# Three sums over partitions: one f32 product replaced by two products of rounded parts

## The chip, the core and the metric

The kernel runs on one core of one Trainium2 chip, as one launch. The metric is the device time of that launch in microseconds; three runs of the kernel before gave 1331.88 to 1332.85 us, median 1332.03 us. The core has five engines that work side by side and meet only at semaphores: PE (TensorE, matrix products), ACT (ScalarE), DVE (VectorE), POOL (GpSimd) and SP (SyncE, which here does nothing but issue DMAs). Each engine takes its instructions strictly in the order in which they stand in its list, so an instruction that waits holds up everything behind it on that engine.

## The reference, cut to what matters

Two layers over a residual stream x of 1024 tokens by 1024 channels, in float32:

```python
for i in range(2):
    h = rms_norm(x, norm_g[i])
    x = x + (conv_branch(h) if i == 0 else attention_branch(h))
    gate = sigmoid(rms_norm(x, ple_norm_g[i]) @ ple_w_gate[i])   # embedding gate
    x = x + (p[i] @ ple_w_proj[i]) * gate

def rms_norm(x, g):
    return x * rsqrt(mean(x * x, axis=-1) + 1e-6) * g
```

There are five mean squares over the channels: the input norm of layer 0 and of layer 1, the norm of each of the two embedding gates, and the layer norm inside the convolution branch (with a mean beside it). The change concerns three: the two gates' and layer 1's input norm.

## The kernel before, in words

The kernel keeps x channel-major: 8 tiles of 128 channels (partitions) by 1024 tokens. A mean square over channels is then a sum over tiles (adds of squares into one 128x1024 tile, on POOL and DVE) followed by a sum over the 128 partitions. That last sum is a product on PE with a 128x128 matrix of ones, which also broadcasts the result to all partitions. `ones_sum` (L186) does it in two halves of 512 tokens. The ones are the right half of the constant tile `cst` (128x256 f32, identity and ones side by side); its load is one of five in `consts` (L363).

All large products are done with operands split in two rounded parts: `hi_of` (L165, ACT) rounds a tile to the type fp32r, `lo_of` (L171, or L173 with a scale; DVE or POOL) subtracts that from the original, and `gemm_k` (L175) multiplies hi·hi, hi·lo and lo·hi on PE (L181). The sums over partitions were the exception: they multiply f32 tiles as they are.

The program goes through these stages: the convolution branch's input product (`bacc`, `aacc`; weights `wraw` and `raw`, input tiles `xt`), the depthwise convolution, its output product (`oacc`), the gate of layer 0 (`gacc`, one unit for each of 8 output tiles; sum `ssb2` in `ple_stat`, L694), layer 1's attention (its first tile of work, products `pqk` and `pv` of weights `raww`, runs before the norm `rstd1`, L819, whose sum is `ssb3`), the attention's output product (`oacc3`), and the gate of layer 1 (sum `ssb4`).

What sets the order: the lists of PE, ACT, DVE and POOL are written out by the code. In the convolution stages and at the gates, `Order` (L116) collects small functions with a due time each and runs them sorted by it; within a function the instructions stand as written. The constants come at -8, ahead of the first weight split at T_X - 1. SP's list alone is ordered by a scheduler, which puts each load where it expects its buffer to be free. Buffers come from pools by tag: the tag X has 8 buffers of 128x1024 at layer 0's gate (`pt`, `pj`, `xi`, `rt`, `rb3` and the squares take them in turn) and 7 at layer 1's.

At a gate, `rstd` (L200) turns the sum into a reciprocal root (DVE L205, ACT's logarithm and exponential L206 and L207, DVE L209 to L215), and `ple` (L712) evicts each unit: DVE multiplies the product by it (L715), ACT takes the sigmoid (L716), DVE multiplies by the projected embedding `pj` (L718), POOL adds x (`xi`, L719), ACT and DVE split the result (`h2hi`, `h2lo`). The logarithm and the sigmoid need different tables on ACT, so an ACT_TABLE_LOAD stands ahead of each.

Of the kernel before, what the change touches and what calls it, by code (L numbers as in the profile page):

```python
# [11 lines left out]
F32 = mybir.dt.float32  # L12
F32R = mybir.dt.float32r
# [9 lines left out]
P = 128  # L23
S = 1024
# [15 lines left out]
    pe=[0, 0, 1, 0, 1, 0, 1, 0],  # L40
# [56 lines left out]
TB, PB = 4, 3  # L97
# [14 lines left out]
def f(ap):  # L112
    return ap.bitcast(F32)
# [18 lines left out]
def kernel(ctx: ExitStack, tc: tile.TileContext, a, out):  # L132
    nc = tc.nc
    act, dve, pool, pe = nc.scalar, nc.vector, nc.gpsimd, nc.tensor
    ctx.enter_context(tc.manual_schedule(engines={ENG.PE, ENG.Activation, ENG.DVE, ENG.Pool}))

    cp = ctx.enter_context(tc.tile_pool(name="const", bufs=1))
# [10 lines left out]
    cst = cp.tile([P, 2 * P], F32, name="cst")  # L148
    vec = cp.tile([P, 7, KT], F32, name="vec")
    ident, ones = cst[:, :P], cst[:, P:]  # L150
    r1 = cp.tile([P, 24], F32, name="r1")
    r64 = cp.tile([P, 24], F32, name="r64")
    ct = cp.tile([P, 24, 2, 16], F32, name="ct")
# [3 lines left out]
    def dma(dst, src):  # L157
        nc.sync.dma_start(dst, src)
# [4 lines left out]
    def hi_of(hi, src, scale=None):  # L163
        if scale is None:
            act.activation(hi, src, AF.Copy)  # L165
        else:
            act.activation(hi, src, AF.Copy, scale=scale)

    def lo_of(lo, src, hi, scale=None, eng=None):
        if scale is None:  # L170
            (eng or dve).tensor_sub(lo, src, f(hi))  # L171
        else:
            dve.scalar_tensor_tensor(lo, src, scale, f(hi), op0=ALU.mult, op1=ALU.subtract)  # L173
# [10 lines left out]
    halves = [slice(0, 512), slice(512, S)]  # L184
    whole = [slice(0, S)]

    def ones_sum(mk, *xs):

        accs = []
        for c in halves:  # L190
            acc = mk()
            for i, x in enumerate(xs):
                pe.matmul(acc, ones, x[:, c], start=i == 0, stop=i == len(xs) - 1)
            accs.append(acc)
        return accs

    def hv(x):
        return [x[:, h] for h in halves]

    def rstd(rb, accs, t, xm, out=None):  # L200

        act.preload_act_table_set("natural_log_exp_and_others")
        both = list(zip(rb, accs, t, xm))
        for r, acc, t, x in both:
            dve.tensor_scalar(x, acc, 1.0 / D, EPS, op0=ALU.mult, op1=ALU.add)  # L205
            act.activation(t, x, AF.Ln)  # L206
            act.activation(r, t, AF.Exp, scale=-0.5)  # L207
        for r, acc, t, x in both:
            dve.tensor_mul(t, r, r)  # L209
        for r, acc, t, x in both:  # L210
            dve.tensor_mul(t, t, x)
        for r, acc, t, x in both:
            dve.tensor_scalar(t, t, -0.5, 1.5, op0=ALU.mult, op1=ALU.add)
        for (r, acc, t, x), y in zip(both, out or rb):
            dve.tensor_mul(y, r, t)  # L215
# [21 lines left out]
    def chunk(o, t, mk, w, xh, xl, nk, dt=1.3, ready=None):  # L237

        acc = {}
        for k in range(nk):  # L240
            def step(k=k):
                if k == 0:
                    acc["a"] = mk()
                gemm_k(acc["a"], (w["h"], w["l"]), xh, xl, k, nk)
            if ready:
                t = max(t, ready[k] - k * dt)
            o.at(t + k * dt, step)
        return t + nk * dt, acc
# [21 lines left out]
    def tok(x, g, t):  # L270

        if g == 0:
            b, c = divmod(t, 4)
            return x.rearrange("p (l c a b) -> p l c a b", l=8, c=4, b=2)[:, :, c, :, b]
        if g == 1:
            r, b = divmod(t, 2)
            return x[:, 256 * r + b : 256 * r + 256 : 2]
        return x[:, t * P : t * P + P]
# [5 lines left out]
    def n_half(x, h):  # L284

        return (x[:, 512 * h : 512 * h + 512].rearrange("p (c l a) -> p c l a", c=4, l=8),
                lambda y: y.rearrange("p (l c a b) -> p c l a b", l=8, c=4, b=2)[..., h])
# [5 lines left out]
    xp = l0.enter_context(tc.tile_pool(name="xp", bufs=1))  # L293
    wp = l0.enter_context(tc.tile_pool(name="wp", bufs=1))
# [7 lines left out]
    def G(name, dt=F32):  # L302
        return gp.tile([P, S], dt, name=name, tag="G", bufs=16)

    def X(name, n=S):
        return xp.tile([P, n], F32, name=name, tag="X", bufs=8)

    def mm(name):
        return ps.tile([P, S], F32, name=name, tag="mm", bufs=2)

    def half(name):
        return ps.tile([P, 512], F32, name=name, tag="half", bufs=2)
# [3 lines left out]
    parts = [{}, {}]  # L316
# [33 lines left out]
    def p_out(i, n, acc, eng):  # L350
        r = X("pout") if i else G("pout")
        eng(r, acc)
        dma(proj_d[i][n], r)
# [9 lines left out]
    def consts():  # L363
        rv["all"] = carry.tile([P, S], F32, name="rope", tag="c")
        at_ = 0
        for nm, n in (("pos", 24), ("invf", 8), ("ggk", 2 * HD), ("posf", 24), ("ang", 192), ("n1", 192), ("n2", 192), ("sin", 192)):
            rv[nm] = rv["all"][:, at_ : at_ + n]
            at_ += n
        rv["pos"] = rv["pos"].bitcast(I32)
        rv["ggk"] = rv["ggk"].rearrange("p (a b) -> p a b", a=2)  # L370
        dma(cst, a["cst"])
        dma(dw, a["dw"])
        for nm in ("pos", "invf", "ggk"):
            dma(rv[nm], a[nm])
# [86 lines left out]
    def stat0():  # L461
        rstd(hv(rb0), ones_sum(lambda: half("ssb"), sv["q", 0]), hv(X("rt")), hv(sv["q", 0]))
# [5 lines left out]
    t = T_X + 2.5  # L468
    T_y = []
    for n in range(KT):  # L470
        if n in P_AT:
            i = P_AT.index(n)
# [14 lines left out]
        dt = 1.3 if n else 2.8  # L487
# [106 lines left out]
    def mean():  # L594
        sv["mb"] = ones_sum(lambda: half("mb"), sv["s1"], dch[7])
# [60 lines left out]
    for n in range(KT):  # L656

        tn = T_o
        if n < 2:
            w = weights(o, wp, a["w_cout"][n], KT, T_o + 4 * n, dve)  # L660
            te, acc = chunk(o, tn + 0.1 * n, (lambda: mm("oacc")) if n else (lambda: hv(ps.tile([P, S], F32, name="oacc0", tag="eA", bufs=1))),
                            w, yh, yl, KT, 2.6, ready)
            if n:
                T_o = te
        else:
            w = weights(o, wp, a["w_cout"][n], KT, tn)
            te, acc = chunk(o, tn, lambda: mm("oacc"), w, yh, yl, KT)
# [24 lines left out]


    def ple_stat(mk, X, s):  # L694
        acc = ones_sum(mk, s["q", 0])
        s["rb"] = X("rb3")
        rstd(hv(s["rb"]), acc, hv(X("rt")), hv(s["q", 0]))

# [27 lines left out]
    for n in range(KT):  # L726
        tn = T_e + C * n + (1.8 if n else 0)
        w = weights(o, wp, a["w_pg"][0, n], KT, tn)
        te, acc = chunk(o, tn, lambda: mm("gacc2"), w, gh, gl, KT)
# [31 lines left out]
    wk = tc.alloc_tile_pool(name="wk", bufs=1, side="right", reuse_waits="tile")  # L761
# [7 lines left out]
    def wk_k(w, raw, eng=None):  # L769

        hi, lo = (wk.tile(list(raw.shape), F32R, name=f"wk{p}", tag=f"wk{next(slot) % WKB}", bufs=1) for p in "hl")
        if eng:
            eng.tensor_copy(hi, raw)
        else:
            hi_of(hi, raw)
        w[0].append(hi)
        w[1].append(lo)
        return lambda eng=dve: lo_of(lo, raw, hi, eng=eng)
# [3 lines left out]
    for k in range(KT):  # L782
        if k > 4:
            raws[k] = wk_raw(a["w_ain"][0], 768, k)
        lo = wk_k(w, raws[k])
# [31 lines left out]
    rbg = s3["q", 0]  # L817

    def rstd1():  # L819

        for acc, c in zip(ones_sum(lambda: pt_("ssb3", "t", TB), rbg), halves):
            dve.tensor_scalar(rbg[:, c], acc, 1.0 / D, EPS, op0=ALU.mult, op1=ALU.add)
        m = pt_("ms", "t", TB, (P, 24))
        row = [kp.tile([1, 512], F32, name="row", tag="P", bufs=PB) for _ in range(2)]
        for h in range(2):
            act.copy(row[h].rearrange("p (c l a) -> p c l a", c=4, l=8), n_half(rbg, h)[1](rbg[0:1]))
        for g in (2, 1, 0):
            for t in range(8):
                x = tok(rbg[0:1], g, t) if g else row[t // 4][:, t % 4 * P : t % 4 * P + P]
                pe.transpose(m[:, 8 * g + t : 8 * g + t + 1], x, ident[0:1, 0:1])  # L830
        act.activation(r64, m, AF.Ln)
        act.activation(r1, r64, AF.Exp, scale=-0.5)
        dve.tensor_mul(r64, r1, r1)
        dve.tensor_mul(r64, r64, m)
        dve.tensor_scalar(r64, r64, -0.5, 1.5, op0=ALU.mult, op1=ALU.add)
        dve.tensor_mul(r1, r1, r64)
        dve.tensor_mul(r64, r1, r1)
        dve.tensor_scalar(r64, r64, 1.0 / HD, None, op0=ALU.mult)
# [42 lines left out]
    def pt_(name, tag, bufs, shape=(P, 512)):  # L881
        return pa.tile(list(shape), F32, name=name, tag=tag, bufs=bufs)
# [318 lines left out]
    for c in range(24 * (NT - 1) + max(place.values()) + 1):  # L1201
        i, k, j = c // 24, c % 24 // 3, c % 3
        if i < NT and c % 24 == 0:
            hh, g, s = order[i]
# [15 lines left out]
        if c == 23:  # L1220
            rstd1()
# [19 lines left out]
        if (i, k) in late:  # L1241
            lo, eng = late.pop((i, k))
# [53 lines left out]
    for tk in "w0 f2 y0 f4 y1 f4 w1 y2 f4 y3 f4 a0 a1 z0 a2 z1 a3 z2 z3".split():  # L1296
        x, n = tk[0], int(tk[1:])
# [23 lines left out]
    wp = tc.alloc_tile_pool(name="wp2", bufs=1, side="right", reuse_waits="tile")  # L1321
    ps = lst.enter_context(tc.tile_pool(name="ps2", bufs=1, space=PSUM, reuse_waits="tile"))

    def X(name):
        return wp.tile([P, S], F32, name=name, tag="X", bufs=7)

    def mm(name):
        return ps.tile([P, S], F32, name=name, tag="mm", bufs=2)
# [7 lines left out]
    for n in range(KT):  # L1336
# [5 lines left out]
        te, acc = chunk(o, tn, lambda: mm("oacc3"), w, yh, yl, 4)  # L1342
# [20 lines left out]
    for n in range(KT):  # L1363
        tn = T_e + C * n + (1.8 if n else 0)
        w = weights(o, wp, a["w_pg"][1, n], KT, tn)
        if n < 7:
            te, acc = chunk(o, tn, lambda: mm("gacc4"), w, gh, gl, KT)
# [6 lines left out]
        else:  # L1374
            ends, acc = chunk_halves(o, tn, lambda: half("gacc4"), w, gh, gl, KT)
# [108 lines left out]
```

## Time and profile before

| | |
|---|---|
| median of three runs | 1332.03 us (1331.88 to 1332.85) |
| the profiled execution's own time | 1330.63 us |
| its span, first to last instruction | 1328.8 us |
| mean granted TensorE clock | 0.985 |
| busy share: PE, DVE, ACT, POOL | 95%, 75%, 52%, 49% |
| chain that ended last, by engine | PE 55%, DVE 17%, POOL 10%, issue 9%, ACT 5%, DMA 2% |

The busy share says that PE is the resource that the whole program is close to; the chain of work that ended last says that only some half of the span is decided by PE itself, and the rest by what PE waited for. Both are averages over stages with different limits, so what follows is read stage by stage: from the timelines of single engines, the table of busy time by stretch and the chain in order of time. Starts are microseconds from the span's start; a value in square brackets is the idle time before an instruction and what ended it.

### The profile page before, as it was taken

How to read it: one execution, taken by the hardware profiler on the slowest of the kernel's cores; microseconds unless marked ns; L12 is line 12 of the kernel's file. 1: busy time of each engine (PE TensorE's matmuls, PEld its weight loads, DVE VectorE, ACT ScalarE, POOL GpSimd, SP SyncE). 2: the span in 40 equal slices, each digit the busy share in tenths (PEclk: the TensorE clock that was granted, in tenths of full speed). 3: DMA queues.
4: the chain of work that ended last, by engine and by line, in shares of the span. 5: the costliest groups of instructions: out<-in, count | busy, mean ns of one | idle time of the engine just before them, and what ended most of it. 6: DMA issues, size and time to landing. Idle time of an engine off the chain costs nothing.

```text
span 1328.8 us, 18960 instructions
## 1 busy us (share of the span) xinstructions
PE 1264.1 (95%) x6440; PEld 1045.4 (79%) x6440; DVE 999.1 (75%) x2036; ACT 688.7 (52%) x1514; POOL 646.0 (49%) x742
## 2 busy tenths in 40 slices
PE   7999999999789999899998899999799999999998
PEld 5878788876578788788887798887699888768786
DVE  6899999995865355668888878888977888774522
ACT  6565555555533333456557567555556666424411
POOL 3679999992644256323324324315522424246342
PEclk9999999999899999899999899999999999999999
DMA  7134120212133345412212212122311312217453
GB/s 280 48 111 143 72 105 31 67 49 76 32 127 143 145 172 183 159 25 61 60 49 62 75 30 71 44 71 90 109 25 25 96 31 64 57 47 259 170 205 127
DMA packets 50356, 126.02 MB, mean 95 GB/s; under 512 B 6188, under 2 KB 19700, under 8 KB 50260
## 3 DMA queue, kind: packets, MB, share of 16 engines
q1 hardware_dynamic: 46804, 112.23, 25.7%
q10 hardware_dynamic: 3456, 12.58, 2.4%
q8 instruction: 51, 0.84, 0.2%
q14 instruction: 45, 0.37, 0.1%
HBM read 83.70 MB, written 26.41 MB: 83 GB/s over the span
## 4 chain that ended last, share of the span: by engine, by line
PE 55%; DVE 17%; POOL 10%; issue 9%; ACT 5%; DMA 2%; SPq 0%; POOLq 0%; DVEq 0%; ACTq 0%
PE pqk L910 15%; PE oacc L181 9%; PE pv L911 8%; PE gacc L181 7%; POOL cc L548 6%; PE po L1056 2%; PE bacc L181 2%; DVE eA L565 2%; DVE oB L565 2%; PE tq L1038 2%; PE tp L970 1%; PE pacc L347 1%; DVE wkl L171 1%; PE gacc L1169 1%; POOL pt L719 1%
## 5 line engine op out<-in xcount | busy, mean ns | idle before, releaser
L910 PE MATMUL pqk<-wkh,h2n 128*128 128x512 f32 x512 | 203.9, 411 | 0.0
L548 POOL TENSOR_TENSOR cc<-cc,tt 128x512 f32<-128x512 f32 x120 | 171.8, 1432 | 20.3 <-ACT tt L547 13.0
L940 POOL TENSOR_TENSOR fh<-fh 128x8 f32<-128x8 f32 x48 | 10.1, 209 | 283.8 <-ACT fh L936 283.8
L911 PE MATMUL pv<-wkh,h2n 128*128 128x256 f32 x512 | 144.9, 283 | 0.0
L547 ACT ACTIVATE tt<-eo,dws 128x512 f32<-128x512 f32 x120 | 85.2, 721 | 76.3 <-POOL cc L548 76.3
L910 PEld LDWEIGHTS pqk<-wkh,h2n 128*128 128x128 f32 x512 | 98.4, 192 | 19.8 <-issue 2.4
L171 POOL TENSOR_TENSOR wl<-raw,wh 128x1024 fp32r<-128x1024 f32 (+1 forms) x37 | 85.7, 2316 | 47.1 <-ACT wh L165 47.1
L910 PE MATMUL pqk<-wkl,h2n 128*128 128x512 f32 x256 | 104.9, 410 | 0.0
L1032 ACT ACTIVATE pt<-pt,stt 128x128 f32<-128x128 f32 (+1 forms) x192 | 85.1, 444 | 35.5 <-DVE stt L1024 34.1
L911 PEld LDWEIGHTS pv<-wkh,h2n 128*128 128x128 f32 x512 | 98.5, 192 | 0.0
L565 DVE SCALAR_TENSOR_TENSOR eA<-ypad,dw,eA 128x513 f32<-128x513 f32 x120 | 89.7, 748 | 0.0
L171 DVE TENSOR_TENSOR ring<-tp,ring 64x256 fp32r<-64x256 f32 x96 | 40.6, 422 | 58.3 <-ACT ring L165 47.6
L1062 ACT COPY ot<-po 64x128 f32<-64x128 f32 x192 | 49.1, 256 | 60.5 <-PE po L1056 59.2
L565 DVE SCALAR_TENSOR_TENSOR oB<-ypad,dw,oB 128x512 f32<-128x512 f32 x104 | 77.6, 746 | 0.0
L911 PE MATMUL pv<-wkl,h2n 128*128 128x256 f32 x256 | 72.4, 283 | 0.0
L719 POOL TENSOR_TENSOR pt<-pt,xi 128x1024 f32<-128x1024 f32 x14 | 33.6, 2400 | 74.4 <-DVE pt L718 45.8
L165 ACT ACTIVATE qq<-tp 64x256 fp32r<-64x256 f32 x96 | 36.3, 378 | 61.6 <-PE tp L970 60.9
L165 ACT ACTIVATE wh<-raw 128x1024 fp32r<-128x1024 f32 (+1 forms) x52 | 51.9, 998 | 21.5 <-issue 11.8
L1056 PE MATMUL po<-pp,vv 128*128 128x256 f32 x280 | 51.5, 292 | 11.1 <-DVE pp L171 11.0
L1072 DVE TENSOR_TENSOR og<-po,ot 64x128 f32<-64x128 f32 x192 | 54.5, 284 | 6.0
L1070 DVE TENSOR_TENSOR ot<-po,ot 64x128 f32<-64x128 f32 x192 | 55.2, 288 | 4.6
L910 PEld LDWEIGHTS pqk<-wkl,h2n 128*128 128x128 f32 x256 | 49.1, 192 | 9.0 <-issue 0.9
(287 smaller groups left out, 3822.9 us busy)
## 6 DMA issues: line engine op xcount, KB each, us to landing
raww<-in_w_ain_dram SPq DMA_DIRECT2D x48, 384.0 KB
ring<-ring SPq DMA_DIRECT2D x96, 128.0 KB
raw<-in_w_cin_dram SPq DMA_DIRECT2D x22, 512.0 KB
proj_d<-pout SPq DMA_DIRECT2D x16, 512.0 KB
x_d<-x ACTq DMA_DIRECT2D x16, 512.0 KB
raw<-in_w_pg_dram SPq DMA_DIRECT2D x16, 512.0 KB
pj<-proj_d SPq DMA_DIRECT2D x16, 512.0 KB
xi<-x_d SPq DMA_DIRECT2D x16, 512.0 KB
```

Of the source, the lines that this page charges most:

```text
L165: act.activation(hi, src, AF.Copy)
L171: (eng or dve).tensor_sub(lo, src, f(hi))
L181: pe.matmul(dst, w_[:, k, :], x[k][:, sl], start=(k == 0 and i == 0 and j == 0), stop=(k == nk - 1 and i == 1))
L547: act.activation(tt, src, AF.Copy, scale=w)
L548: pool.tensor_add(sv["c", n], sv["c", n], tt)
L565: dve.scalar_tensor_tensor(acc, src, w, acc, op0=ALU.mult, op1=ALU.add)
L910: pe.matmul(self.pqk, x, ww[:, :512], start=a0, stop=a1)
L911: pe.matmul(self.pv, x, ww[:, 512:], start=a0, stop=a1)
L1032: act.activation(x, x, AF.Exp, scale=-1.0, bias=nm, accum_out=den)
L1056: pe.matmul(po[:, h], vv, self.pp[pr][:, b, h], start=b == 0, stop=b == self.nk - 1)
L1070: dve.tensor_add(t, self.po[pr][pp[h], h, 0], t)
L1072: dve.tensor_add(tok(self.u.og[pr][pp[h]], self.g, self.s), *(runs(x, self.g) for x in (self.po[pr][pp[0], h, 1], self.ot[pr][pp[h]])))
```

## The change

`ones_sum2` takes the place of `ones_sum` at three sites: the two gates' `ple_stat` and layer 1's `rstd1`. It splits the tile of squares into hi and lo (each half of 512 tokens: one ACT instruction, one DVE instruction) and multiplies both with `ones_r`, a copy of the ones in fp32r. So two f32 products become four of fp32r, with two more instructions on ACT and two more on DVE at each site. The sums of layer 0's input norm and of the convolution's layer norm stay as they were. The copy `ones_r` is one ACT instruction, written in `consts` between the load of `cst` and that of `dw`. The parts take buffers of tag X at the gates (`qhi`, `qlo`) and of tag raww in layer 1 (`rbgp`).

```diff
+    ones_r = cp.tile([P, P], F32R, name="ones_r")
...
+    def ones_sum2(mk, x, hi, lo):
+
+        accs = []
+        for i, c in enumerate(halves):
+            hi_of(hi[i], x[:, c])
+            lo_of(lo[i], x[:, c], hi[i])
+            accs.append(mk())
+            for part in (hi, lo):
+                pe.matmul(accs[i], ones_r, part[i], start=part is hi, stop=part is lo)
+        return accs
...
         dma(cst, a["cst"])
+        act.copy(ones_r, ones)
         dma(dw, a["dw"])
...
     def ple_stat(mk, X, s):
-        acc = ones_sum(mk, s["q", 0])
+        acc = ones_sum2(mk, s["q", 0], *(hv(X(f"q{p}", dt=F32R)) for p in ("hi", "lo")))
...
     def rstd1():
 
-        for acc, c in zip(ones_sum(lambda: pt_("ssb3", "t", TB), rbg), halves):
+        parts = [[wk.tile([P, 512], F32R, name="rbgp", tag=f"raww{2 * q + h}", bufs=1) for h in range(2)] for q in range(2)]
+        for acc, c in zip(ones_sum2(lambda: pt_("ssb3", "t", TB), rbg, *parts), halves):
```

The line numbers of the changed kernel are 1 to 14 higher than those of before.

ACT's list at the start of the program, before (the `wh` are the first rounded weights, the `hhi` the first rounded input tiles; DMAHW and a number name the semaphore of one of eight lanes that SP's loads take in turn):

```order
L165 ACT_TABLE_LOAD
L165 ACTIVATE wh<-wraw 128x512 [waits DMAHW0_49]
L167 ACTIVATE hhi<-xt,vec 128x1024 [waits DMAHW2_49,DMAHW1_49]
L455 ACTIVATE sq<-xt 128x1024
L165 ACTIVATE wh<-wraw 128x512 [waits DMAHW3_49]
```

and now:

```order
L384 ACT_TABLE_LOAD
L384 CAST ones_r<-cst 128x128 [waits DMAHW5_49]
L166 ACTIVATE wh<-wraw 128x512 [waits DMAHW0_49]
L168 ACTIVATE hhi<-xt,vec 128x1024 [waits DMAHW2_49,DMAHW1_49]
L468 ACTIVATE sq<-xt 128x1024
```

The copy stands first of ACT's work, ahead of the first weight split, and waits for the lane of the `cst` load.

SP's list from the `cst` load on, before:

```order
L158 DMA cst<-in_cst_dram 128x256 [waits DMAHW5_49]
L158 DMA dw<-in_dw_dram 128x248 [waits DMAHW6_49]
L158 DMA rope<-in_pos_dram 128x24 [waits DMAHW7_49]
L158 DMA rope<-in_invf_dram 128x8 [waits DMAHW0_49]
L158 DMA rope<-in_ggk_dram 128x128 [waits DMAHW1_49]
L158 DMA raw<-in_w_cin_dram 128x1024 [waits DMAHW2_49,Pool_49]
L158 DMA raw<-in_w_cin_dram 128x1024 [waits DMAHW3_49,Pool_49]
L158 DMA praw<-in_pT_dram 128x1024 [waits DMAHW4_49]
L158 DMA praw<-in_w_pp_dram 128x1024 [waits DMAHW5_49]
```

and now:

```order
L159 DMA cst<-in_cst_dram 128x256 [waits DMAHW5_49]
L159 DMA dw<-in_dw_dram 128x248 [waits DMAHW6_49]
L159 DMA rope<-in_pos_dram 128x24 [waits DMAHW7_49]
L159 DMA rope<-in_invf_dram 128x8 [waits DMAHW0_49]
L159 DMA rope<-in_ggk_dram 128x128 [waits DMAHW1_49]
L159 DMA praw<-in_pT_dram 128x1024 [waits DMAHW2_49]
L159 DMA praw<-in_w_pp_dram 128x1024 [waits DMAHW3_49]
L159 DMA praw<-in_pT_dram 128x1024 [waits DMAHW4_49]
L159 DMA praw<-in_w_pp_dram 128x1024 [waits DMAHW5_49]
L159 DMA raw<-in_w_cin_dram 128x1024 [waits DMAHW6_49,Pool_49]
L159 DMA raw<-in_w_cin_dram 128x1024 [waits DMAHW7_49,Pool_49]
```

The scheduler has put four loads for the embedding projection (`praw`) ahead of the second pair of convolution weights (`raw`). At the switch to layer 1 it has likewise put `mask`, `misc` and `sel2f` behind the eighth of twelve `raww` loads instead of behind the twelfth.

ACT's list at the gate of layer 0, from the last weight split before the sum to the first sigmoid's result, before:

```order
L165 ACTIVATE wh<-raw 128x1024 [waits DMAHW0_49,PE_49,Pool_49]
L202 ACT_TABLE_LOAD
L206 ACTIVATE rt<-sq_2889 128x512 [waits DVE_49,Pool_49]
L207 ACTIVATE rb_3392<-rt 128x512 [waits DMAHW1_49,Activation_49]
L206 ACTIVATE rt<-sq_2889 128x512 [waits DVE_49]
L207 ACTIVATE rb_3392<-rt 128x512 [waits Activation_49]
L165 ACTIVATE wh<-raw 128x1024 [waits DMAHW4_49,PE_49,Pool_49]
L716 ACT_TABLE_LOAD
L716 ACTIVATE pt<-pt 128x1024 [waits DVE_49]
```

and now:

```order
L166 ACTIVATE wh<-raw 128x1024 [waits DMAHW0_49,PE_49,Pool_49]
L166 ACTIVATE qhi<-sq_2891 128x512 [waits DVE_49]
L166 ACTIVATE qhi<-sq_2891 128x512
L214 ACT_TABLE_LOAD
L218 ACTIVATE rt<-sq_2891 128x512 [waits DVE_49,Pool_49]
L219 ACTIVATE rb_3402<-rt 128x512 [waits DMAHW5_49,Activation_49]
L218 ACTIVATE rt<-sq_2891 128x512 [waits DVE_49]
L219 ACTIVATE rb_3402<-rt 128x512 [waits Activation_49]
L166 ACTIVATE wh<-raw 128x1024 [waits DMAHW4_49,PE_49]
L729 ACT_TABLE_LOAD [waits DMAHW1_49,DVE_49]
L729 ACTIVATE pt<-pt 128x1024 [waits PE_49]
```

Two splits stand ahead of the logarithm's table load. The first evicted tile `pt` now takes a buffer that a part had, its sigmoid waits for PE as well, and the wait for DVE's multiplication (L728) has moved from the sigmoid to the table load ahead of it.

## Rows read from the trace of the kernel before

**Rows 1.** Busy time by stretch: stretch, length, each engine's busy us and instructions, clock, DMA share, GB/s.
```profile
31.00:330.00 299.00, 294.48 (x1242) 232.33 (x1241) 269.58 (x363) 165.62 (x210) 241.44 (x156) 1.00 0.23 78
```

**Rows 2.** Timeline of ACT, start: start us, us, engine, line, operation, tiles, [idle <-releaser].
```profile
3.23 0.63 ACT L165 ACTIVATE wh<-wraw 128x512 fp32r<-128x512 f32 x1 [1.23 <-DMA wraw<-in_w_cin_dram]
6.00 1.15 ACT L167 ACTIVATE hhi<-xt,vec 128x1024 fp32r<-128x1024 f32 x1 [2.15 <-DMA xt<-in_xT_dram]
...
19.59 1.06 ACT L165 ACTIVATE wh<-raw 128x1024 fp32r<-128x1024 f32 x1 [1.97 <-DMA raw<-in_w_cin_dram]
```

**Rows 3.** Timeline of SP's queue, start: when each load was issued.
```profile
0.72 0.39 SPq L158 DMA_DIRECT2D wraw<-in_w_cin_dram  x1
...
4.10 4.20 SPq L158 DMA_DIRECT2D xt<-in_xT_dram  x6
8.65 0.33 SPq L158 DMA_DIRECT2D cst<-in_cst_dram  x1
...
14.74 1.60 SPq L158 DMA_DIRECT2D raw<-in_w_cin_dram  x2
17.27 0.33 SPq L158 DMA_DIRECT2D praw<-in_pT_dram  x1
17.65 0.42 SPq L158 DMA_DIRECT2D praw<-in_w_pp_dram  x1
```

**Rows 4.** Timeline of PE, start.
```profile
7.20 1.22 PE L181 MATMUL bacc<-hhi,wh 128*128 128x512 f32 x2 [7.20 <-ACT hhi L167]
...
20.61 0.63 PE L181 MATMUL bacc<-hhi,wh 128*128 128x512 f32 x2
...
23.41 0.63 PE L181 MATMUL bacc<-hhi,wh 128*128 128x512 f32 x2
...
27.19 0.63 PE L181 MATMUL bacc<-hhi,wh 128*128 128x512 f32 x2
```

**Rows 5.** Timeline of POOL, start.
```profile
11.20 4.40 POOL L171 TENSOR_TENSOR wl<-wraw,wh 128x512 fp32r<-128x512 f32 x2 [1.22 <-ACT wh L165]
```

**Rows 6.** The chain that ended last, in order of time, last gate: start us, us, what.
```profile
1244.74 1.72 PE ssb L193 x4
1246.45 65.94 PE gacc L181 x288
```

**Rows 7.** Timeline of PE at layer 0's gate.
```profile
457.57 1.88 PE L193 MATMUL ssb<-sq,cst 128*128 128x512 f32 x4
```

**Rows 8.** Timeline of DVE at layer 0's gate.
```profile
451.04 1.22 DVE L686 TENSOR_TENSOR sq<-sq,sq 128x1024 f32<-128x1024 f32 x1
...
465.73 1.22 DVE L715 TENSOR_TENSOR pt<-gacc,rb 128x1024 f32<-128x1024 f32 x1
```

**Rows 9.** Timeline of ACT at layer 0's gate.
```profile
462.86 1.28 ACT L716 ACT_TABLE_LOAD   x1
466.99 1.06 ACT L716 ACTIVATE pt<-pt 128x1024 f32<-128x1024 f32 x1 [2.84 <-DVE pt L715]
```

**Rows 10.** Timeline of PE at the end of layer 0's gate.
```profile
542.14 0.58 PE L911 MATMUL pv<-wkh,h2hi 128*128 128x256 f32 x1 [4.06 <-DVE pt L715]
```

**Rows 11.** Timeline of DVE at layer 1's norm.
```profile
550.12 1.97 DVE L794 TENSOR_TENSOR ss<-ss,sq 128x1024 f32<-128x1024 f32 x1 [0.84 <-ACT sq L750]
...
554.67 0.69 DVE L822 TENSOR_SCALAR ss<-ssb 128x512 f32<-128x512 f32 x1 [0.17 <-PE ssb L193]
```

**Rows 12.** Timeline of ACT at layer 1's norm.
```profile
555.45 0.40 ACT L1219 CAST sel<-sel2f 72x256 fp32r<-72x256 f32 x1 [4.14 <-DVE ss L822]
555.76 1.21 ACT L826 COPY row<-ss 1x512 f32<-1x512 f32 x2
```

**Rows 13.** Timeline of SP's queue at the switch to layer 1.
```profile
528.08 23.28 SPq L158 DMA_DIRECT2D raww<-in_w_ain_dram  x12
...
552.96 0.45 SPq L158 DMA_DIRECT2D sel2f<-in_sel_dram  x1
```

**Rows 14.** Timeline of DVE at layer 1's gate.
```profile
1237.84 1.22 DVE L1358 TENSOR_TENSOR sq<-sq,sq 128x1024 f32<-128x1024 f32 x1
```

More of the change, by code (lines that the diff above doesn't have):

```diff
@@ L303, in G, with X @@
         return gp.tile([P, S], dt, name=name, tag="G", bufs=16)
-    def X(name, n=S):
-        return xp.tile([P, n], F32, name=name, tag="X", bufs=8)
+    def X(name, n=S, dt=F32):
+        return xp.tile([P, n], dt, name=name, tag="X", bufs=8)
     def mm(name):
@@ L1322, with X @@
     ps = lst.enter_context(tc.tile_pool(name="ps2", bufs=1, space=PSUM, reuse_waits="tile"))
-    def X(name):
-        return wp.tile([P, S], F32, name=name, tag="X", bufs=7)
+    def X(name, dt=F32):
+        return wp.tile([P, S], dt, name=name, tag="X", bufs=7)
     def mm(name):
```

## The prediction, made before the changed kernel was run

> **What bounds the kernel now.** I read three views, in this order. The table of busy time by stretch says where PE is the limit: in the convolution stage it worked 294.48 of 299 us at full clock, and only 4.5 us are idle [rows 1]. Whatever delays the start of that stage is therefore not made up inside it. The timelines of ACT, SP and PE say what the start itself hangs on: the reader is to see that ACT had its first weight at 3.23, waited 2.15 us for the first `xt`, rounded it at 6.00 [rows 2], and that PE began at 7.20, released by just that instruction [rows 4]. The chain in order of time, with the timelines of the gates, says what each of the three sums is worth: at layer 1's gate PE runs without a gap, so the sum's 1.72 us stand on the path [rows 6]; at layer 0's gate the evictions decide, since at its end PE waited 4.06 us for DVE's L715 [rows 10].
>
> **The sums themselves.** Two f32 products took 1.72 us at layer 1's gate, and 288 fp32r products of the same size 65.94 us, or 0.229 each [rows 6]. Four of these are 0.92 us, so PE gets 0.80 us back per site. The price is two ACT roundings of 128x512 (0.63 us each, as the first weight split of that size [rows 2]) and two DVE subtractions (0.69 us for an instruction of that size [rows 11]). In a row, first hi, second hi, second lo are 0.63 + 0.63 + 0.69 = 1.95 us before the last product can run.
>
> **Layer 1's gate.** The squares are complete at 1237.84 + 1.22 = 1239.06 [rows 14], and PE comes to the sum at 1244.74 [rows 6]. The 1.95 us lie in these 5.7 us; were that cover gone, they would cost up to 1.95 less 0.80. PE bounds this stage: **-0.8 us** (bounds -0.8 and +1.2).
>
> **Layer 0's gate.** The squares are complete at 452.26 [rows 8], PE comes at 457.57 [rows 7]; again 5.3 us hide the parts. But here the eviction of eight units in a row decides, each unit's instructions on DVE, ACT and POOL behind the one before. What counts is when the first `pt` passes. The reciprocal root starts from the first half of the sum, which is now done after two products (0.46) instead of one (0.86): 0.4 us earlier, and ACT's four instructions pace the rest. Against that, the sigmoid's table load, 1.28 us, ran at 462.86, long before `pt` was ready at 465.73 + 1.22 = 466.95 [rows 8, 9]. In the new order the load itself waits for DVE's multiplication. So `pt` is ready at 466.55, the load ends at 467.85, and the sigmoid starts 0.86 us later than its 466.99 [rows 9]. I carry this through all eight units: **+0.9 us**. Bounds: -0.8 (PE decides after all and keeps its gain) and +1.3 (the load in full).
>
> For this table load the trace has 1.28 us. The Trainium skill, page "ScalarE: Activation LUTs", section "What ACT_TABLE_LOAD costs", gives about 2.7 us with the drain. By it this term would be 2.3 and the whole time 1.4 us longer; the measurement decides, and nothing below uses the page's figure.
>
> **Layer 1's norm.** Nothing covers the parts here: the squares are complete at 550.12 + 1.97 = 552.09 [rows 11], and PE has nothing else. Then hi, hi, lo end at 554.04, the last product at about 554.3, and with 0.2 to hand over and 0.69 on DVE the second half is done at 555.2, against 554.67 + 0.69 = 555.36 [rows 11]. The gain on PE pays for the parts. The next step, two row copies on ACT, began at 555.76 because the cast of `sel2f` stood before them [rows 12]; that load was issued at 552.96, behind twelve `raww` loads that waited for buffers until 551.4 [rows 13]. Now it follows the eighth, so the cast can run before the parts and the copies start at once: **-0.3 us**. Bounds: -1.0 and +0.6. The four `raww` loads moved behind it are for the next unit of work, some tiles later; I cost that at nothing.
>
> **The start.** This is the large term. The copy `ones_r` stands first on ACT and waits for `cst`. Behind it on ACT stand every `wh` and `hhi`, and on them wait POOL's `wl`, DVE's `hlo` and all of PE. `cst` is issued at 8.65, behind all eight `xt`, and lands by 17.65, when the load that takes its lane next went out [rows 3]. The `xt` loads ahead of it were still moving: the last one's lane was free at 17.27, when `praw` went out [rows 3]; 128 KB behind them can hardly land before some 17.5. With 17.6, 0.3 for the copy (a cast of 72x256 took 0.40 [rows 12]) and 0.6 for the first weight, the first `hhi` starts at 18.5 instead of 6.00: 12.5 us later. The 2.15 us wait for `xt` is not paid again, as all `xt` are there; nor can ACT catch up, as it ran without a gap from 6.00 to the wait before 19.59 [rows 2].
>
> One stall goes. In the sixth step of the product PE took 27.19 - 23.41 = 3.78 us where the step before took 2.80 [rows 4], because ACT had waited 1.97 us for `raw` [rows 2]. Now `raw` goes out behind four `praw`, once POOL has done the first of its pair of `wl`: before at 11.20 + 2.2 = 13.4 [rows 5], now at 25.9. It took 4.85 us from 14.74 to 19.59, behind `xt` [rows 2, 3], and 2.5 us is the shortest landing seen (0.72 to 3.23 [rows 2, 3]); so it lands between 28.4 and 30.75. ACT needs it at 19.59 - 1.97 + 12.5 = 30.1. Between all of the 0.98 us and some of it is recovered; I take 0.7. The start: 12.5 - 0.7 = **+11.8 us**, and by rows 1 the 299 us behind it shift with it. Bounds: +12.6 (no recovery, a copy of 0.4) and, if `cst` landed as fast as the first load, at 8.65 + 2.5 = 11.15, a first `hhi` at 12.05: 6.05 - 0.7 = +5.4.
>
> That the early end is not the one I take rests on the row at 17.27: `cst` was queued behind four `xt` that were still to land. The Trainium skill says two things here, on the page "DMA: Bandwidth & Descriptors". Its section "Anatomy of one DMA — SWDGE (gpsimd) path" prices a transfer at 2.0 us and its bytes at 436 GB/s, which would land `cst` at 10.95 and give 1337. Its section "Queues, rings and completion order" says that each DMA engine takes descriptors in the order of its ring, which gives the later landing. The trace agrees with the second: the loads' lanes come free in order of issue.
>
> **Sum.** 11.8 + 0.9 - 0.3 - 0.8 = +11.6 us. The profiled execution took 1330.63, so it would take 1342.2; the median of the runs is 1.40 above it, so **1343.6 us**.
>
> **Rivals.**
> - `cst` lands early, because the 16 DMA engines share out their time among loads in flight. For it: it is a quarter the size of an `xt` load. Against: 17.27 and 17.65 [rows 3]. Time: 1332.0 + 5.4 - 0.2 = 1337.2.
> - `sel2f` comes no earlier than before. Then the cast at 555.45 stands ahead of the parts on ACT, and the parts begin at 555.85 instead of 552.09: their end at 558.95 and the copies at 559.0, 3.3 us after 555.76. For it: the cast is ahead in ACT's list. Against: eight loads are waited for, not twelve. Time: 1343.6 + 3.3 + 0.3 = 1347.2.
> - Not slower: the late start is swallowed, because what follows the first product is paced by something that does not wait for ACT, such as POOL's and DVE's depthwise convolution being late anyway. POOL has 241 and DVE 270 busy us in the stretch [rows 1], so neither is the one limit, but both start from ACT's output too, and the idle 4.5 us of PE cannot hold 12.5. It decides only if a slack of over 12 us lies behind the start. Then the sums alone count: 1332.0 - 0.3 - 0.8 and -0.8 to +0.9 at layer 0's gate: 1330 to 1332.
> - The change does what it says on PE, and the table load's wait costs nothing: 1342.7, within the forecast's own range.
>
> **How the numbers follow.** The forecast has 0.80, within 1341 to 1346; `cst` early, or in between, 0.10; `sel2f` late 0.05; swallowed 0.05. The likeliest gives 1343.6. The range from 1336.5 to 1347 takes in the early landing and nearly reaches the late `sel2f`. A difference of 0.2%, 2.7 us, is what a measurement of this kernel tells from no change. The swallowed start, 1330 to 1332, is mostly within 0.2%: faster 0.02, same 0.04, slower 0.94.
>
> **What would show it.** In the changed kernel's profile the first `wh` starts at some 17.9 behind the copy, with an idle time of some 15 us before the copy put down to `cst`; PE's first product comes at 19.7; the sixth step has lost most of its 0.98 us stall. The sum at each gate takes 0.9 us on PE; the sigmoid's table load of layer 0's gate ends just before the first sigmoid. The row copies at layer 1's norm come some 0.3 us sooner, counted from the squares. The forecast is wrong if the copy runs before 15, if PE's stretch behind the start holds more idle time before than I read, or if the gates move by over 2 us.

## The result, and the profile after

The changed kernel took **1346.05 us** (median of four runs, 1344.83 to 1346.71) beside 1331.95 for the kernel before on the same chip (four runs, 1331.78 to 1332.85): a ratio of 1.0105, interval 1.009 to 1.012, slower by 14.1 us. The forecast was 1343.6. The profiled execution took 1346.31 us, with a span of 1344.5; that of before took 1330.63 with 1328.8. The two profiles are therefore 15.7 us apart and the medians 14.1, because the profiled execution of before was 1.3 us under its median.

In the two profiles I followed one event after the other. Each row is the start of the same instruction in both timelines:

| event | before | after | later by |
|---|---|---|---|
| PE, first product | 7.20 | 20.21 | 13.0 |
| PE, sum of the input norm | 31.39 | 44.86 | 13.5 |
| PE, sum of the convolution's norm | 316.50 | 331.22 | 14.7 |
| PE, sum of layer 0's gate | 457.57 | 472.28 | 14.7 |
| DVE, last `pt` of that gate | 540.81 | 556.35 | 15.5 |
| PE, first `pqk` of layer 1 | 557.36 | 572.82 | 15.5 |
| PE, sum of layer 1's gate | 1244.58 | 1259.31 | 14.7 |
| DVE, last `pt` of that gate | 1323.42 | 1338.83 | 15.4 |

Four places move: the start (+13.5), the convolution (+1.2), layer 0's gate (+0.8) and layer 1's gate (+0.7). Attention gave 0.7 back in this profile; in the profiles of the experiments below the same stretch lay between 1.6 us under and 0.2 us over that of before.

**The start.** ACT's timeline of after (columns as in [rows 2]):

```profile
18.29 0.30 ACT L384 CAST ones_r<-cst 128x128 fp32r<-128x128 f32 x1 [16.29 <-DMA cst<-in_cst_dram]
18.50 0.62 ACT L166 ACTIVATE wh<-wraw 128x512 fp32r<-128x512 f32 x1
19.03 1.13 ACT L168 ACTIVATE hhi<-xt,vec 128x1024 fp32r<-128x1024 f32 x1
...
30.53 1.04 ACT L166 ACTIVATE wh<-raw 128x1024 fp32r<-128x1024 f32 x1
```

Against [rows 2], ACT stands idle 16.29 us for the copy's source, and the first `hhi` moves from 6.00 to 19.03. The wait for `raw` of 1.97 us is gone (the row at 30.53 has no idle time). SP's queue says when the loads went out:

```profile
9.15 0.33 SPq L159 DMA_DIRECT2D cst<-in_cst_dram  x1
...
17.95 0.33 SPq L159 DMA_DIRECT2D praw<-in_pT_dram  x1
18.32 0.43 SPq L159 DMA_DIRECT2D praw<-in_w_pp_dram  x1
```

`cst` went out 0.5 later than in [rows 3], and the second `praw` load, which takes its lane, 0.7 later. PE's timeline of after:

```profile
20.21 1.22 PE L182 MATMUL bacc<-hhi,wh 128*128 128x512 f32 x2 [20.21 <-ACT hhi L168]
...
25.18 1.05 PE L182 MATMUL aacc<-hhi,wl 128*128 128x512 f32 x2
26.03 0.85 PE L182 MATMUL bacc<-hhi,wh 128*128 128x512 f32 x2
...
31.85 0.63 PE L182 MATMUL bacc<-hhi,wh 128*128 128x512 f32 x2
...
34.65 0.63 PE L182 MATMUL bacc<-hhi,wh 128*128 128x512 f32 x2
...
37.86 0.63 PE L182 MATMUL bacc<-hhi,wh 128*128 128x512 f32 x2
```

and PE's timeline of before, where the slow pairs end:

```profile
10.39 1.05 PE L181 MATMUL aacc<-hhi,wh 128*128 128x512 f32 x2
11.25 0.66 PE L181 MATMUL aacc<-hlo,wh 128*128 128x512 f32 x2
```

The sixth step takes 37.86 - 34.65 = 3.21 us instead of the 3.78 of [rows 4], so 0.57 of the stall came back. But the pairs that take 1.05 run until about 26.0, 5.8 us after the first product; in before it was 11.25, after 4.05 us. The row at 31.85, one step (2.80) ahead of 34.65, is at the full pace again. That the slow pairs ran at the lower of TensorE's two levels is inferred from their pace: pairs behind the gap of the next paragraph, where the granted clock was 0.53, take the same 1.05, but for the start itself the table of busy time prints 1.00 in both kernels.

**The convolution.** Its depthwise part begins in every kernel with a PE gap of 3.3 to 3.4 us that ends on DVE. The busy time by stretch right behind that gap (columns as in [rows 1]), in after:

```profile
166.40:170.00 3.60, 3.60 (x9) 2.86 (x10) 3.60 (x6) 1.20 (x2) 3.52 (x3) 0.53 0.38 149
```

and the same view of before:

```profile
152.90:157.00 4.10, 4.08 (x18) 3.39 (x19) 4.10 (x7) 2.10 (x4) 3.94 (x4) 1.00 0.34 132
```

The granted clock was 0.53 in after and 1.00 in before, and PE did 9 products in 3.60 us instead of 18 in 4.10. ACT's next eviction waited for these products until 171.05, and ACT's next tile for POOL's chain, `tt`, stood behind it. POOL's timeline of after shows its wait for that tile:

```profile
172.82 2.67 POOL L561 TENSOR_TENSOR cc<-cc,tt 128x512 f32<-128x512 f32 x2 [1.25 <-ACT tt L560]
```

By the end of the stage 1.2 us were lost.

**Layer 0's gate.** DVE's timeline of after, with its first two `pt`:

```profile
480.05 1.23 DVE L728 TENSOR_TENSOR pt<-gacc,rb 128x1024 f32<-128x1024 f32 x1
...
490.86 1.21 DVE L728 TENSOR_TENSOR pt<-gacc,rb 128x1024 f32<-128x1024 f32 x1
```

ACT's timeline of after, with the first sigmoid:

```profile
481.34 1.28 ACT L729 ACT_TABLE_LOAD   x1 [4.18 <-issue]
482.63 1.06 ACT L729 ACTIVATE pt<-pt 128x1024 f32<-128x1024 f32 x1
```

and DVE's timeline of before, with the second `pt`:

```profile
475.15 1.21 DVE L715 TENSOR_TENSOR pt<-gacc,rb 128x1024 f32<-128x1024 f32 x1
```

Counted from the sum, the first `pt` is 0.4 earlier than in [rows 8], yet the table load starts only when it is done, and the sigmoid comes 0.93 later than in [rows 9]. The second `pt` is 1.0 later (490.86 - 472.28 = 18.58 against 475.15 - 457.57 = 17.58).

**Layer 1's norm.** PE's timeline of after, with twelve one-column products that turn the row, and the first `pqk`:

```profile
570.98 1.36 PE L844 MATMUL ms<-cst,ss 1*128 1x1 f32 x12 [0.20 <-DVE ss L836]
572.82 0.80 PE L924 MATMUL pqk<-wkh,h2hi 128*128 128x512 f32 x1
```

and PE's timeline of before, with the same twelve products:

```profile
555.42 1.36 PE L830 MATMUL ms<-cst,ss 1*128 1x1 f32 x12 [0.45 <-DVE ss L822]
```

DVE's timeline of after, with the last sum of squares and the two halves of `ss`:

```profile
565.39 2.20 DVE L807 TENSOR_TENSOR ss<-ss,sq 128x1024 f32<-128x1024 f32 x1 [0.59 <-ACT sq L763]
...
569.63 1.30 DVE L836 TENSOR_SCALAR ss<-ssb 128x512 f32<-128x512 f32 x2
```

ACT's timeline of after, with the cast and the row copies:

```profile
566.60 0.41 ACT L1233 CAST sel<-sel2f 72x256 fp32r<-72x256 f32 x1
...
570.96 1.22 ACT L840 COPY row<-ss 1x512 f32<-1x512 f32 x2 [2.18 <-DVE ss L836]
```

The cast is out of the way early, the two copies and PE's products are let go by the same `ss`, and PE's are the ones that `pqk` follows.

**Layer 1's gate.** The chain in order of time of after:

```profile
1248.48 10.99 PE gacc L182 x48
1259.47 0.93 PE ssb L206 x4
1260.40 67.20 PE gacc L182 x288
```

The sum takes 0.93 instead of 1.72 [rows 6], and the 288 products behind it, which the change does not touch, 67.20 instead of 65.94.

### The profile page after: what moved, and what is told of

The parts are those of the page before. It is cut to its first block, busy times and chain, and to the rows that moved or that the text cites. A ratio compares the mean times of both kernels' runs of the same rounds, so it can differ in the third digit from the quotient of the medians.

```text
span 1344.5 us, 18980 instructions
## 1 busy us (share of the span) xinstructions
PE 1268.0 (94%) x6440; PEld 1048.5 (78%) x6440; DVE 1007.8 (75%) x2042; ACT 692.6 (52%) x1521; POOL 645.5 (48%) x742
## 4 chain that ended last, share of the span: by engine, by line
PE 60%; DVE 19%; POOL 8%; issue 6%; ACT 4%; DMA 2%; SPq 1%; POOLq 0%; DVEq 0%; ACTq 0%
PE pqk L924 14%; PE gacc L182 13%; PE oacc L182 9%; PE pv L925 7%; POOL cc L561 4%; DVE eA L578 2%; DVE oB L578 2%; PE bacc L182 2%; PE po L1070 2%; PE tq L1052 2%; DVE wkl L172 2%; PE tp L984 1%; PE pacc L359 1%; DMA raww<-in_w_ain_dram 1%; PE gacc L1183 1%
## 5 line engine op out<-in xcount | busy, mean ns | idle before, releaser
L182 PE MATMUL bacc<-hhi,wh 128*128 128x512 f32 x128 | 41.0, 402 | 20.2 <-ACT hhi L168 20.2
```

Source lines behind the costliest of these rows:

```text
L182: pe.matmul(dst, w_[:, k, :], x[k][:, sl], start=(k == 0 and i == 0 and j == 0), stop=(k == nk - 1 and i == 1))
```

## The experiments

In all that say "copy late", `ones_r` is copied with the input norm's sum, just ahead of its table load on ACT (at 32.44 in the first of them), and the copy waits for nothing. Where a time is called a single run, the kernel ran once and so did the one beside it, if no more is said; 27 runs of before, beside the first experiments, lay between 1330.15 and 1335.02, so there the rows decide and not the time.

### The copy moved back

```diff
-        act.copy(ones_r, ones)
...
+    at(T_S - 0.5, lambda: act.copy(ones_r, ones))
     at(T_S, stat0)
```

> All three sums in two parts as in the changed kernel, but the copy of the ones stands on ACT behind the first eight input tiles instead of ahead of the first weight. Theory (nearly all the loss is ACT's wait for cst at the start): the first hhi starts at 6.0 again, PE begins at 7.2, the first sum comes at 31.4, and the time is 1332 with only the three sums' own terms left: +1.0 at layer 0's gate, -0.1 at the norm, -0.6 to +0.7 at layer 1's gate, so 1332.3 to 1333.6. Rival (splitting the sums costs much of it): 1336 or more, with the gates' evictions over 3 us later than before.

Measured: 1332.47 us (1332.11 to 1334.79) beside 1331.9, ratio 1.0005 [0.9997, 1.0014]. PE began at 7.49, released by `hhi`, and the input norm's sum came at 31.69: the start is back within 0.3 of before. Layer 0's gate still cost 0.8, layer 1's norm 0.2, layer 1's gate 0.7. The three sums in parts are worth no more than the measurement can tell; the place of the copy is the loss.

### The copy alone

The copy stays first; the sums go back to f32.

```diff
-        acc = ones_sum2(mk, s["q", 0], *(hv(X(f"q{p}", dt=F32R)) for p in ("hi", "lo")))
+        acc = ones_sum(mk, s["q", 0])
...
-        for acc, c in zip(ones_sum2(lambda: pt_("ssb3", "t", TB), rbg, *parts), halves):
+        for acc, c in zip(ones_sum(lambda: pt_("ssb3", "t", TB), rbg), halves):
```

> The copy of the ones stands first on ACT as in the changed kernel, but all three sums are the f32 products of before, so nothing reads the copy. Theory: the start alone is 13.0 us of wait, 1.0 of products at the low clock level, less 0.6 for the raw stall that goes, so +13.5, and +1.25 more if the products at the depthwise convolution drop to the low clock level again: 1345.4 to 1346.7. Rival (the sums cost a good part): under 1344.

Measured: 1344.53 us (1343.25 to 1345.38), ratio 1.0091 [1.0077, 1.0105], a little under what I expected. An unused copy of 0.30 us, in this place, costs 12.6 us, against 14.1 for the whole change. The copy ran at 18.25, PE began at 20.18.

### Where `cst` stands in the queue

The same kernel as after, with the load of `cst` issued first of all:

```diff
-        dma(cst, a["cst"])
         act.copy(ones_r, ones)
...
+    at(-9.1, lambda: dma(cst, a["cst"]))
```

> As the changed kernel, with the copy first on ACT, but the load of cst is issued first of all loads instead of behind the eight input tiles. Theory (the wait is as long as the loads queued ahead of cst): the copy runs at about 3.2 to 3.8, all input loads are 0.3 us later, PE begins at 7.5 to 8.0; 1332 + 0.5 + 0.3 for the sums = 1332.5 to 1334. Rival (the copy's place on ACT costs of itself, a table load or a drain): PE begins at 10 or later, 1335 or more.

Measured: 1333.42 us, ratio 1.0012 [1.0003, 1.0021]. ACT's timeline of this kernel:

```profile
2.89 0.30 ACT L383 CAST ones_r<-cst 128x128 fp32r<-128x128 f32 x1 [0.90 <-DMA cst<-in_cst_dram]
...
6.56 1.15 ACT L168 ACTIVATE hhi<-xt,vec 128x1024 fp32r<-128x1024 f32 x1 [2.14 <-DMA xt<-in_xT_dram]
```

The copy is still first on ACT, and the loss is gone: it now fits into the wait for the first `xt`, and what remains of the start is 0.56 us (6.56 against 6.00), because one more load stands ahead of `xt`.

Then with `cst` behind five of the eight `xt`:

```diff
-        dma(cst, a["cst"])
         act.copy(ones_r, ones)
...
+    at(-8.4 + 0.045, lambda: dma(cst, a["cst"]))
```

> As the changed kernel, but the load of cst stands behind five of the eight input tiles instead of all eight. Theory (cst lands when what is queued ahead of it has landed; each input tile is 1.28 us): the copy starts at 18.3 - 3 x 1.28 = 14.5, PE at 16.4, first sum at 41. Rival (loads in flight share the engines, and cst lands a fixed time after its issue, 9.1 us in the changed kernel's profile): issued at some 5, it would land at 14 too, but with cst first (issued at 0.7) the copy would have run at 9.8, not at 2.9; a copy before 12 would speak for a fixed time of a few us and against the queue.

Measured: 1343.15 us in a single run, beside 1332.52. ACT's timeline of this kernel:

```profile
14.21 0.30 ACT L383 CAST ones_r<-cst 128x128 fp32r<-128x128 f32 x1 [12.20 <-DMA cst<-in_cst_dram]
...
14.95 1.14 ACT L168 ACTIVATE hhi<-xt,vec 128x1024 fp32r<-128x1024 f32 x1
```

`cst` was issued at 6.42, and the copy ran 7.8 us later; with the load issued first, at 0.72, it was 2.2. With none, five or eight `xt` ahead the copy ran at 2.89, 14.21 and 18.29: it lands later the more stands ahead of it in the queue, and not a fixed time after its issue. The Trainium skill, "DMA: Bandwidth & Descriptors", section "Queues, rings and completion order", says that each DMA engine takes the descriptors of one ring in order; these three rows agree with it.

### Layer 1's gate alone

Copy late, the other two sums in f32:

```diff
-        acc = ones_sum2(mk, s["q", 0], *(hv(X(f"q{p}", dt=F32R)) for p in ("hi", "lo")))
+        acc = ones_sum2(mk, s["q", 0], *(hv(X(f"q{p}", dt=F32R)) for p in ("hi", "lo"))) if s is not s2 else ones_sum(mk, s["q", 0])
```

> Only layer 1's gate takes its sum in two parts; the copy of the ones is late on ACT, the other two sums are f32. Theory (PE gets the 0.8 us back and nothing else moves): 1331.2, the products behind the sum at 0.229 us each. Rival (the products behind the fp32r sum run at 0.233 each, as in the changed kernel's profile, because the f32 sum no longer stands there): 0.8 is more than eaten by 336 times 0.0043 = 1.4, so 1332.6.

Measured: 1332.59 us, ratio 1.0002 [0.9993, 1.0011]. The interval holds both expected times; the chain of this kernel at the gate tells them apart:

```profile
1245.23 0.93 PE ssb L206 x4
1246.15 67.20 PE gacc L182 x288
```

The slower products come with the parts at this one site. In the kernel with the copy alone, whose sum is f32, the chain has the old figures:

```profile
1259.58 1.72 PE ssb L194 x4
1261.29 65.94 PE gacc L182 x288
```

My first idea was the order of the four products, two in a row into one accumulator. With hi, hi, lo, lo instead of hi, lo, hi, lo:

```diff
         for i, c in enumerate(halves):
...
-            for part in (hi, lo):
+        for part in (hi, lo):
+            for i in range(2):
                 pe.matmul(accs[i], ones_r, part[i], start=part is hi, stop=part is lo)
```

> Only layer 1's gate in two parts, copy late, and the four products of the sum ordered hi, hi, lo, lo, so that two products in a row go to different accumulators, as everywhere else. Theory (the products behind the sum fall from 0.229 to 0.233 us each because two fp32r products in a row went to one accumulator): the 288 products behind the sum take 65.9 us again and the time is 1331.2. Rival (it is the fp32r sum or its weights as such): 67.2 us, as with the order hi, lo, hi, lo.

Measured: 1333.88 us in a single run beside 1332.52, and the chain of this kernel:

```profile
1247.38 0.93 PE ssb L207 x4
1248.31 67.20 PE gacc L182 x288
```

That idea fell.

### Layer 0's gate, with the parts in other buffers

Copy late, only this sum in parts, and the parts in tag H instead of X:

```diff
-        acc = ones_sum2(mk, s["q", 0], *(hv(X(f"q{p}", dt=F32R)) for p in ("hi", "lo")))
+        acc = ones_sum2(mk, s["q", 0], *(hv(H(f"q{p}")) for p in ("hi", "lo"))) if s is s2 else ones_sum(mk, s["q", 0])
```

> Only layer 0's gate in two parts, copy late, and the parts lie in buffers of tag H instead of X, so that the first pt takes the buffer that it had before and the sigmoid's table load stands again without a wait. Theory (of the +1.0 at this gate, the waiting table load is +1.4 and the earlier sum -0.4): the first sigmoid follows its pt at once, all eight pt come 0.4 us earlier than before, counted from the sum, and the time is 1331.5. Rival (the parts themselves, by ACT's and DVE's extra work, cost the 1.0): the second pt comes 1.0 later than before, as in the changed kernel.

Measured: 1331.00 us in a single run beside 1332.52. ACT's timeline of this kernel:

```profile
464.41 1.28 ACT L729 ACT_TABLE_LOAD   x1
468.54 1.06 ACT L729 ACTIVATE pt<-pt 128x1024 f32<-128x1024 f32 x1 [2.84 <-DVE pt L728]
```

The sum ran at 459.50, 1.93 later than in before, and the first `pt` no longer takes a part's buffer. The table load is out of the way again, as in [rows 9], and the last `pt`, at 542.24, is 0.5 earlier than in before, counted from the sum. With the parts in tag X it was 0.8 later. So the cost at this gate was the buffers, not the products.

The same kernel, timed:

> The version the runs point to: only layer 0's gate in parts, in buffers of tag H, copy of the ones late, the other two sums f32. Theory: -0.4 us of before at the gate and nothing else, so 1331.5, which the rounds will hardly tell from before. Rival (the two ACT and two DVE instructions more cost something that the one profile did not show): 1332.5 or more.

Measured: 1331.56 us (1329.44 to 1332.85) beside 1332.79, ratio 0.9988 [0.9979, 0.9997]. The 1.2 us are more than the 0.4 expected, which lies at the end of the interval; the gate itself is 0.55 us shorter in this profile.

### Parts where they pay, an f32 product last

Copy late, layer 0's gate in parts of tag H, the norm in f32, and layer 1's gate with its first half in parts and its second as one f32 product:

```diff
+    def ones_sum2(mk, x, hi, lo, mixed=False):
...
+            if mixed and i:
+                accs.append(mk())
+                pe.matmul(accs[i], ones, x[:, c], start=True, stop=True)
+                continue
```

> Copy late; layer 0's gate in parts that lie in tag H, layer 1's norm f32, and at layer 1's gate the first half of the sum in two fp32r products, the second half in one f32 product, which so stands last before the gate's 288 products. Theory (an f32 product behind the fp32r ones puts the products back to 0.229 us): 65.9 us for the 288. Rival (two fp32r products of the sum are enough, whatever follows): 67.2 us.

Measured: 1329.24 us in a single run beside 1332.79, the median of 15. The chain of this kernel at layer 1's gate:

```profile
1243.83 0.47 PE ssb L210 x2
1244.29 0.86 PE ssb L204 x2
1245.15 65.93 PE gacc L182 x288
```

In these kernels the pace of the 288 products goes with the last product of the sum: f32, 65.93; fp32r, 67.20. Whether the f32 product must be the last, or need only be one of them, is not shown: none of the kernels had it first and the fp32r products behind it. Timed:

> The same kernel as e10_mixed, now timed. Theory: -0.4 at layer 0's gate and 1.72 - 1.33 = -0.4 at layer 1's gate, so 0.8 under before: ratio 0.9994, within what the rounds can tell. Rival (its one time of 1329.24 was not chance, and something else in it saves some 3 us): ratio 0.998 or less.

Measured: 1330.34 us (1328.76 to 1333.1) beside 1332.27, ratio 0.9986 [0.9977, 0.9994]. It is faster than both kernels, by 1.9 us against before, which is less than the 0.2% that I set as the bound. Its profile has the two gates' terms as expected, -0.56 and -0.40 us. The measured ratio lies between the two that were expected, with that of the theory at the end of the interval, so the other 1.0 us are not explained.

## Why the prediction was right, and where not

**The start** decided it, as forecast: an instruction that needs nothing of the first product stood first on ACT and waited for a load at the end of the queue. The copy alone costs 12.6 us, and with `cst` first in the queue 1.5 are left of the whole change. The size was a little off: +13.5 instead of +11.8. Of these 1.7 us, some 0.5 is the later `hhi` (19.03 against 18.5: `cst` let the copy go at 18.29 and not at 17.6, and the copy and the first weight took 0.74 and not 0.9), 0.1 a smaller part of the stall won back (0.57 against 0.7), and about 1.0 a term that I did not have: PE's slow products at the start ran longer. I do not tie that to the wait. The kernel of the experiment with other buffers, which began at 7.31 like before, had slow products to 13.9, and the one with `cst` in the middle of the queue to 22.8, 6.7 us after its first.

**The convolution** had no term and took 1.2. It is no part of the change's cost that I can show: the kernel with `cst` first, whose start is 0.6 off before's, has a granted clock of 0.59 at this place, and the one with the copy late 1.00. The busy time by stretch behind the gap, with `cst` first:

```profile
153.50:156.70 3.20, 3.20 (x9) 2.51 (x10) 3.20 (x6) 1.21 (x2) 3.12 (x3) 0.59 0.43 168
```

and the same view with the copy late:

```profile
153.30:156.70 3.40, 3.40 (x15) 2.83 (x16) 3.40 (x6) 1.40 (x3) 3.32 (x3) 1.00 0.40 159
```

The copy's place does not explain it, and what decides between the two stays open. The twelve profiles show one thing more: before, the one with the copy late and the one with layer 1's gate alone, whose first products were slow for some 4.0 us, have 1.00 in the 3.4 us behind the gap and lose nothing from the input norm's sum to the convolution's. The other nine, whose first products were slow for 5.7 to 6.7 us, have 0.50 to 0.60 there and lose 1.1 to 1.7 us. Six of these nine began within 0.8 us of before. So the slow start and the slow convolution go together, and no run here shows either to be the copy's doing.

**Layer 0's gate** came as the working said (+0.8 against +0.9, by way of the table load), and the other buffers, which take the load's wait away, turn it into -0.5.

**Layer 1's norm** was forecast at -0.3 and came at 0.0. The cast did run ahead (566.60, before the squares end at 565.39 + 2.20 = 567.59), and the row copies came 0.3 sooner counted from the squares: 3.37 us, against 555.76 - 552.09 = 3.67 [rows 11, 12]. The step that failed is "the copies start at once", taken for the end of the path: PE's twelve one-column products start at 570.98 from the same `ss`, 15.56 later than the 555.42 of before, and `pqk` follows them. The copies were not on the path. The parts, too, cost a little more than taken: the second half of `ss` was done 569.63 + 1.30 - 567.59 = 3.34 us after the squares, where the working had 555.2 - 552.09 = 3.1 and before 3.27.

**Layer 1's gate** was forecast at -0.8 and came at +0.7. The working "PE bounds this stage: -0.8" held for the sum (-0.79), and took the 288 products behind it for constant. They went from 0.229 to 0.2333 us each: +1.26, and the two halves of the last chunk 0.2 more.

**The rivals.** The early `cst` fell: the copy ran at 18.29. The late `sel2f` fell with the cast at 566.60 (its 3.3 us should have been 559.0 - 555.76 = 3.2). The swallowed start fell: the 13 us are in every row of the table. The free table load fell by 0.93. In all, the terms off are +1.7, +1.2, -0.1, +0.3 and +1.5; attention's -0.7 and the last output's +0.3, which I did not follow up, lead to the 15.7 of the profiles. Against the median the forecast was only 2.45 us too low, since it added the 1.40 us by which before's median lay above its profiled execution, while after's lies 0.26 below. That much of the closeness is luck, and 1346.05 lies just above the 1341 to 1346 that the prediction gave its own mechanism.

## What to carry to other kernels

A conversion of a constant is work for an engine that runs in order: everything behind it waits as long as the constant's load stands in its queue, here 16.29 us for a copy of 0.30 us. Put it next to its first use, or its load first. When new tiles take buffers of an existing tag, look at who inherits them: a wait can move onto an instruction ahead of the one that needs it, here a table load. A shorter sum on the path counts only if what follows it keeps its pace; read the mean time of the products around it, too.

## What the runs showed of the hardware that I had not expected

Products of one shape and type ran at two paces behind layer 1's sum. In before, with the copy alone and in the other kernels with an f32 sum or an f32 product last, 288 took 65.93 or 65.94 us (0.229 each); in the six whose sum there was all fp32r, 67.20 (0.233). The 48 ahead of the sum took 10.99 in each. An f32 product in front is not enough, since at layer 0's gate products took 0.233 behind an f32 sum too (294 in 68.62 us, in the kernel with layer 1's gate alone). The cause stays open.

After a gap of the same length, 3.3 to 3.4 us, the granted clock of the next products was 1.00 in three kernels (before, copy late, layer 1's gate alone) and 0.50 to 0.60 in the other nine, with the same kind of products ahead of the gap. It was 1.00 in just those kernels whose first products of all had been slow for the shortest time.
